# A hybrid decoder layer on one core: where the additions of the early down-projection chunks stand, when a third block sum is split, and which later chunks use seven products

## The chip, the cores and the metric

One core of one Trainium2 chip. The metric is the device time of one launch in microseconds (us), taken as the median of several executions; before the change it is 1123.89 us (three executions, 1123.33 to 1124.59). The profile is one further execution, recorded by the hardware profiler.

## The reference

One decoder layer on `x` of 256 tokens by 2048 features, float32:

```
proj = h @ w_in                                  # 2048 x 6144
a_out = diff_attention(8 heads); b_out = moba_attention(8 heads)   # with 256 tokens: causal attention
h = layer_norm(alpha * h + concat(a_out, b_out) @ w_out)
u = h @ w_up;  g, val = u[:, :5632], u[:, 5632:]
f = (silu(conv_b + causal 3-tap depthwise conv(g)) * val) @ w_down # 5632 x 2048
h = layer_norm(alpha * h + f)
```

The change concerns the last matrix product, `act @ w_down`, and the additions that bring its result into the residual.

## The kernel before

**Precision.** Every float32 operand of a large product is split into a high part `hi` (ScalarE copies it to the matmul format) and a low part `lo` (VectorE subtracts, `lo = x - hi`); a product is then hi·hi + hi·lo + lo·hi. So each weight tile costs one copy on ScalarE (ACT) and one subtraction on VectorE (DVE) before TensorE (PE) can use it.

**Stages.** Values, then queries, keys and attention, then the output projection and the first norm; then 88 *units* of the up projection (a unit is one 128-wide column of `w_up`: even ones gate, odd ones value; counted from 0, `i - first_u` in the code), then 14 *down chunks* at the end and the last norm. Instructions are written out by hand in one order per engine; each engine takes its own list in order and waits on semaphores.

**A unit** (`up_step`). PE does 16 pairs of matmuls (512 and 256 columns wide) into one bank, `bank[3]`. Then it does a slice of a *down job* (below). At the unit's end ACT copies the bank out (`up_copy`, tile `ub`, L1175); the next unit's first matmul writes the same bank, so it waits for that copy. In the same unit ACT and DVE split the weights of the unit after the next one (`hi` L190, `lo` L198), finish the gate of the unit before (`up_sum` L1184, taps L561/L562, product L568), and prepare the down job's operands.

**A down job.** `w_down` is taken in chunks: 256 of its rows (a pair `p`, 0 to 21) by 1024 of its columns (a half `n`). A chunk's product is a 2x2 by 2x2 block product done in seven block products instead of eight (Strassen's idea in Winograd's form): 21 matmuls of 512 columns, where the ordinary way takes 24. For that DVE forms sums of the weight blocks. Line by line: `tf` L1301 (block 0 minus block 3), `tf` L1309 (3 plus 2), `tf` L1317 (the *third sum*, 2 minus the first), `tf` L1269 (the fourth); each is split into `tslot` (high part by ACT at L803, low part by DVE at L806). The job also needs the plain blocks split (`rslot`, L1362 and L1364) and, for a chunk seen for the first time ("fresh"), sums of the activations (`sf`, split into `sp`, L809 and L812). The list `jobs` gives each job's half, pair, first unit, and its length in units, four or two. The sums of job j+1 are formed while job j runs; its third sum comes in the last unit of job j, behind everything else, just ahead of that unit's copy `ub`.

**Banks of the down jobs.** Each of the seven products adds up over the chunks in its own PSUM bank: MB[5], MB[7], MB[6], MB[1] (banks 5, 7, 6, 4) for the shared ones, and CB[0][0], CB[0][1], CB[1][0] (banks 0, 1, 2). The first ten jobs (`EARLY`) do half n=1 of pairs 0 to 9; then the banks have to be added into the residual `z` and given over to half n=0, all 20 remaining jobs. This handing over is the *flush*. Before the change it is eleven additions on DVE (L1211, L1223, L1226) and one copy on ACT, at the heads of units 46, 47 and 48 (`shared_out(1, ...)` and three additions of the CB banks), and job 10 is four units long (46 to 49), with no products in unit 46 so that the banks can be emptied. Job 9 is two units long (44 and 45).

**The down chunks at the end.** Chunks 0 and 1 are half n=0 of pairs 20 and 21, chunks 2 to 13 are half n=1 of the pairs not done early (index j of the code is the chunk's number minus 2). Chunk by chunk, `begin` splits the weights of the chunk two ahead and loads the one six ahead. The raw weights pass through four tiles in turn, so the load of chunk c+4 can be issued only when chunk c's raw tile is free; SyncE (SP) issues the loads in order. Most chunks are ordinary (24 matmuls); those that the table `SEVEN` names use seven products, whose raw tile is held until `blocks_whole` has read it (L666, L667), after all block sums. Before, these are chunks 5 and 8 (j = 3 and 6). The split tiles hold three ordinary chunks at a time. The last four chunks are taken column by column, all four for one bank, before the next bank.

Of the kernel before, what the change touches and what calls it, by code (L numbers as in the profile page):

```python
# [11 lines left out]
F32 = mybir.dt.float32  # L12
F32R = mybir.dt.float32r
AF = mybir.ActivationFunctionType
ALU = mybir.AluOpType

P = 128
# [29 lines left out]
LATE = 2  # L47

EARLY = 10

SEVEN = {"v": ((), range(1, 8, 3)), "d": (range(PT - LATE), (3, 6))}

ORDER = {"v": (1, 0, 2, 3), "d": (0, 1, 2, 3)}

# [5 lines left out]
def hymba_layer(ctx: ExitStack, tc: tile.TileContext, a: dict):  # L60
# [260 lines left out]
    def at(step, fn, *args, rank=LATER):  # L321
        after.setdefault(step, []).append((rank, len(after.get(step, ())), fn, args))
# [411 lines left out]

    side, raw0 = {}, {}

    jobs = []
    for p in range(EARLY):
        jobs.append((1, p, 4 * p + 8, 2 if p == EARLY - 1 else 4))
    jobs.append((0, 0, 4 * EARLY + 6, 4))  # L740
    for p in range(EARLY, PT - LATE):
        jobs.append((0, p, 4 * p + 10, 2))
        if p - EARLY + 1 < EARLY:
            jobs.append((0, p - EARLY + 1, 4 * p + 12, 2))
    FLUSH = EARLY

    def fresh(j):
        return jobs[j][1] >= EARLY or jobs[j][0] == 1
# [53 lines left out]
    def t_hi(j, f):  # L802
        ACT.activation(side["t"][:, 0, j], f, AF.Copy)  # L803

    def t_lo(j, f):
        DVE.tensor_tensor(side["t"][:, 1, j], f, side["t"][:, 0, j].bitcast(F32), ALU.subtract)  # L806

    def s_hi(j):
        ACT.activation(side["sh"][j], side["s"][j], AF.Copy)  # L809

    def s_lo(j):
        DVE.tensor_tensor(side["sl"][j], side["s"][j], side["sh"][j].bitcast(F32), ALU.subtract)  # L812
# [385 lines left out]
    def cuts(j, u):  # L1198

        _, _, first, length = jobs[j]  # L1200
        if length == 2:
            c = (0, 9, 21)
        elif j == FLUSH:
            c = (0, 0, 7, 14, 21)
        else:
            c = (0, 5, 10, 15, 21)
        return c[u - first], c[u - first + 1]

    def z_add(n, t, c, src):
        s = slice((2 * n + c) * 512, (2 * n + c + 1) * 512)  # L1210
        DVE.tensor_tensor(z[:, t, s], z[:, t, s], src, ALU.add)  # L1211

    def shared_out(n, part, early=False):

        if part == 0:
            kept["u"] = kept["gb"] if early else work.tile([P, 512], F32, name="u", tag="sh", bufs=1)
        u = kept["u"]
        if part == 0:
            ACT.activation(u, MB[1], AF.Copy)
            z_add(n, 0, 1, MB[5])  # L1220
            z_add(n, 1, 1, MB[5])
            z_add(n, 0, 0, u)
            DVE.tensor_tensor(u, MB[6], u, ALU.add)  # L1223
        else:
            z_add(n, 0, 1, u)
            DVE.tensor_tensor(u, MB[7], u, ALU.add)  # L1226
            z_add(n, 1, 0, u)
            z_add(n, 1, 1, u)

    def up_step(i):  # L1230

# [14 lines left out]
        if i > first_u + 2:  # L1246
            u = up_sum(i - 1)
            if s % 2 == 0:
                act_out(f, u)
        if j == FLUSH and 0 in now:  # L1250
            shared_out(1, 0, True)
        if j == FLUSH and 1 in now:
            shared_out(1, 1, True)
        if j == FLUSH and 2 in now:
            for t, c in ((1, 0), (0, 0), (0, 1)):
                z_add(1, t, c, CB[t][c])
        split_hi(i + 2, 0)
        if s % 2 == 1 and u is not None:
            gate_in(f, u)
# [55 lines left out]
        if 3 in nxt:  # L1315
            w = raw_of(j + 1)
            DVE.tensor_tensor(side["f"][0], w[:, 2], side["f"][0], ALU.subtract)  # L1317
            if fresh(j + 1):
                s_hi(0)
            t_hi(2, side["f"][0])  # L1320
            if fresh(j + 1):
                s_lo(0)
            t_lo(2, side["f"][0])
        if i == first_d - 2:
            split_act(first_d, 0)
        if i == first_d - 1:
# [71 lines left out]
    for i in range(first_d, NS - PAIRED_END):  # L1398
        begin(i)
        _, p, n, j = stream[i]  # L1400
        if i == last[0] - 1:
            act_back(last[3])
            ends = (down_slot()[:, 0:8].rearrange("p (a b) c -> p a (b c)", b=2),
                    keep.tile([P, 4, 1024], F32R, name="end", tag="mb"))
            for j, end in zip(last[2:], ends):
                for k in range(2):
                    split(j, k, end)
            for part in range(2):
                shared_out(1, part)
        if seven(i):  # L1410
            mm_seven(i)
        else:
            for k in range(2):
                mm_d(i, 0, [0, 1], k)
            if n == 0 and p == PT - 1:
                for c in range(2):
                    z_add(0, 0, c, CB[0][c])
            elif i < last[0] - 1:
                middle(i)
            for k in range(2):  # L1420
                mm_d(i, 1, [0, 1], k)
            done(i)
            if n == 0 and p == PT - 1:
                for c in range(2):
                    z_add(0, 1, c, CB[1][c])
                middle(i)
                for t in range(2):
                    for c in range(2):
                        at(i + 4 + 3 * t, z_stats, t, c, (512, 256)[t])
        for k in range(2):  # L1430
            aparts.pop((i, k))

# [171 lines left out]
```

## Time and profile before

| | |
|---|---|
| median of three executions | 1123.89 us |
| the profiled execution | 1124.31 us |
| its span, first to last instruction | 1122.5 us |
| PE busy | 1106.5 us (99%) |
| DVE busy | 889.0 us (79%) |
| ACT busy | 692.2 us (62%) |
| mean granted PE clock | 0.995 |
| down jobs: a unit with 9 products, one with 12 | 7.61 us, 8.28 us |

The profiled execution's own time is 1.8 us above its span. In the views, PE is TensorE's matmuls and PEld its weight loads; a row of a timeline gives the start, the duration, engine, line, operation and tiles, and in brackets how long the engine was idle before and what released it. PE's matmuls overlap, and their ends are modelled, so a busy share of 99% does not say that PE lost nothing: lost time is read from the starts of matmuls and from how long a unit took.

### The profile page before, as it was taken

How to read it: one execution, taken by the hardware profiler on the slowest of the kernel's cores; microseconds unless marked ns; L12 is line 12 of the kernel's file. 1: busy time of each engine (PE TensorE's matmuls, PEld its weight loads, DVE VectorE, ACT ScalarE, POOL GpSimd, SP SyncE). 2: the span in 40 equal slices, each digit the busy share in tenths (PEclk: the TensorE clock that was granted, in tenths of full speed). 3: DMA queues.
4: the chain of work that ended last, by engine and by line, in shares of the span. 5: the costliest groups of instructions: out<-in, count | busy, mean ns of one | idle time of the engine just before them, and what ended most of it. 6: DMA issues, size and time to landing. Idle time of an engine off the chain costs nothing.

```text
span 1122.5 us, 15881 instructions
## 1 busy us (share of the span) xinstructions
PE 1106.5 (99%) x5908; PEld 949.5 (85%) x5908; DVE 889.0 (79%) x1470; ACT 692.2 (62%) x1109; POOL 61.8 (6%) x88
## 2 busy tenths in 40 slices
PE   9999999999999999999999999899999999999997
PEld 7888888888888898888888888788888888888876
DVE  6776778877745779888888878888888888886876
ACT  6666666655443577666666666566676666666452
POOL 0000010000000000000000000000000000001003
PEclk9999999999999999999999999999999999999998
DMA  9889866454545447888787888578888777798772
GB/s 344 273 276 325 227 195 201 150 187 156 183 168 200 157 166 264 279 271 277 271 273 262 292 266 286 187 262 300 277 269 267 252 281 269 262 307 284 245 268 76
DMA packets 61884, 273.80 MB, mean 244 GB/s; under 512 B 6304, under 2 KB 7792, under 8 KB 44016
## 3 DMA queue, kind: packets, MB, share of 16 engines
q1 hardware_dynamic: 52592, 233.48, 57.1%
q0 software_dynamic: 9072, 39.06, 15.3%
q8 instruction: 46, 0.75, 0.3%
q10 hardware_dynamic: 144, 0.26, 0.1%
q14 instruction: 30, 0.25, 0.1%
HBM read 231.60 MB, written 18.87 MB: 223 GB/s over the span
## 4 chain that ended last, share of the span: by engine, by line
PE 84%; DVE 8%; ACT 4%; issue 2%; DMA 2%; SPq 0%; ACTq 0%; DVEq 0%
PE bank L279 83%; DVE lo L198 1%; DVE rslot L1364 1%; ACT ub L1175 1%; DMA raw<-in_w_d 1%; ACT rslot L1362 1%; ACT hi L190 1%; DVE z L1211 1%; ACT tslot L803 1%; DVE tf L1309 1%; DVE tf L1317 1%; PE bank L421 0%; DVE lo L181 0%; DMA raw<-in_w_v 0%; DVE gc L562 0%
## 5 line engine op out<-in xcount | busy, mean ns | idle before, releaser
L279 PE MATMUL bank<-h,hi 128*128 128x512 f32 x1376 | 483.5, 392 | 4.7 <-ACT ub L1175 3.6
L279 PE MATMUL bank<-h,lo 128*128 128x256 f32 x1376 | 388.4, 282 | 0.0
L279 PEld LDWEIGHTS bank<-h,hi 128*128 128x128 f32 x1376 | 258.9, 188 | 63.8 <-ACT ub L1175 9.3
L279 PEld LDWEIGHTS bank<-h,lo 128*128 128x128 f32 x1376 | 260.6, 189 | 3.2
L198 DVE TENSOR_TENSOR lo<-raw,hi 128x1024 fp32r<-128x1024 f32 x171 | 207.6, 1220 | 19.8 <-ACT hi L190 19.6
L181 DVE TENSOR_TENSOR lo<-raw,hi 128x1024 fp32r<-128x1024 f32 x133 | 160.3, 1221 | 70.9 <-ACT hi L179 70.1
L179 ACT ACTIVATE hi<-raw 128x1024 fp32r<-128x1024 f32 x141 | 147.6, 1057 | 67.1 <-PE bank L279 46.5
L279 PE MATMUL bank<-x,hi 128*128 128x512 f32 x512 | 182.8, 398 | 0.0
L190 ACT ACTIVATE hi<-raw 128x1024 fp32r<-128x1024 f32 x171 | 178.2, 1050 | 0.0
L279 PE MATMUL bank<-x,lo 128*128 128x256 f32 x512 | 144.1, 282 | 0.0
L803 ACT ACTIVATE tslot<-tf 128x512 fp32r<-128x512 f32 x120 | 74.4, 627 | 76.9 <-DVE tf L1317 35.4
L279 PEld LDWEIGHTS bank<-x,hi 128*128 128x128 f32 x512 | 96.1, 188 | 20.6 <-issue 1.0
L1175 ACT ACTIVATE ub<-bank 128x512 f32<-128x512 f32 x86 | 51.1, 594 | 92.0 <-PE bank L279 92.0
L806 DVE TENSOR_TENSOR tslot<-tf,tslot 128x512 fp32r<-128x512 f32 x120 | 82.0, 690 | 23.2 <-ACT tslot L803 21.3
L279 PEld LDWEIGHTS bank<-x,lo 128*128 128x128 f32 x512 | 96.8, 189 | 0.2
L1184 DVE TENSOR_TENSOR ub<-ub 128x256 f32<-128x256 f32 x86 | 36.3, 422 | 28.1 <-ACT ub L1175 28.0
L279 PE MATMUL bank<-hi,x 128*128 128x512 f32 x208 | 55.9, 391 | 0.1
L279 PEld LDWEIGHTS bank<-hi,x 128*128 128x128 f32 x208 | 38.9, 188 | 8.9 <-ACT hi L210 0.9
L279 PE MATMUL bank<-tslot,sp 128*128 128x512 f32 x180 | 45.9, 391 | 0.0
L279 PE MATMUL bank<-hi,mh 128*128 128x512 f32 x128 | 41.6, 396 | 0.0
L565 ACT ACTIVATE gc<-gc 128x256 f32<-128x256 f32 x44 | 18.4, 418 | 36.8 <-DVE gc L562 36.8
L279 PE MATMUL bank<-lo,mh 128*128 128x512 f32 x128 | 40.8, 390 | 0.0
(246 smaller groups left out, 1532.1 us busy)
## 6 DMA issues: line engine op xcount, KB each, us to landing
raw<-in_w_u SPq DMA_DIRECT2D x88, 1024.0 KB, 6.8
raw<-in_w_qk SPq DMA_DIRECT2D x32, 1024.0 KB, 5.0
raw<-in_w_d SPq DMA_DIRECT2D x58, 512.0 KB, 7.9
raw<-in_w_o SPq DMA_DIRECT2D x16, 1024.0 KB, 4.8
ring<-in_w_d SPq DMA_DIRECT2D x30, 512.0 KB, 8.4
raw<-in_w_v SPq DMA_DIRECT2D x28, 512.0 KB, 7.4
rslot<-ring POOLq DMA_DIRECT2D x15, 768.0 KB, 7.0
dparts<-rslot SPq DMA_DIRECT2D x20, 512.0 KB, 3.8
```

Of the source, the lines that this page charges most:

```text
L179: ACT.activation(hi[:, s], t[:, x:y], AF.Copy)
L181: DVE.tensor_tensor(lo[:, s], t[:, x:y], hi[:, s].bitcast(F32), ALU.subtract)
L190: ACT.activation(hi, t[:, half * 1024:half * 1024 + 1024], AF.Copy)
L198: DVE.tensor_tensor(lo, t[:, half * 1024:half * 1024 + 1024], hi.bitcast(F32), ALU.subtract)
L279: PE.matmul(out, lhsT, rhs, start=start, stop=stop)
L565: ACT.activation(gates[f], gates[f], AF.Silu)
L803: ACT.activation(side["t"][:, 0, j], f, AF.Copy)
L806: DVE.tensor_tensor(side["t"][:, 1, j], f, side["t"][:, 0, j].bitcast(F32), ALU.subtract)
L1175: ACT.activation(t.rearrange("p j t -> p (j t)"), up_bank(i), AF.Copy)
L1184: DVE.tensor_tensor(u[:, 0], u[:, 0], u[:, 1], ALU.add)
L1211: DVE.tensor_tensor(z[:, t, s], z[:, t, s], src, ALU.add)
L1309: DVE.tensor_tensor(side["f"][1], w[:, 3], w[:, 2], ALU.add)
```

## The change

Four things.

1. `jobs`: job 9 is four units long (44 to 47) instead of two, and job 10 two (48 and 49) instead of four. From unit 50 on the jobs stand where they stood.
2. The flush is rewritten as `early_out(0)` to `early_out(3)`, in units 46, 47, 48 (at the end of the unit's list) and 49 (near its head). It has 13 additions on DVE instead of 11 (MB[1] is added to all four quarters of `z` directly, and the running sum `u` starts from a copy of MB[6]) and still one copy on ACT.
3. `third_out`: where job j+1 is two units long, the split of its third sum (and of the fresh job's first activation sum) is not done in the last unit of job j but is carried to the head of the next unit, behind `up_sum` and `act_out`. The sum itself (L1317, now L1335) stays.
4. `SEVEN`: among the end's chunks only chunk 6 (j = 4) uses seven products, not chunks 5 and 8. Two z statistics move one chunk later.

```diff
-SEVEN = {"v": ((), range(1, 8, 3)), "d": (range(PT - LATE), (3, 6))}
+SEVEN = {"v": ((), range(1, 8, 3)), "d": (range(PT - LATE), (4,))}
...
-    jobs = []
+    jobs = [(1, p, 4 * p + 8, 4) for p in range(EARLY)]
     for p in range(EARLY):
-        jobs.append((1, p, 4 * p + 8, 2 if p == EARLY - 1 else 4))
-    jobs.append((0, 0, 4 * EARLY + 6, 4))
-    for p in range(EARLY, PT - LATE):
-        jobs.append((0, p, 4 * p + 10, 2))
-        if p - EARLY + 1 < EARLY:
-            jobs.append((0, p - EARLY + 1, 4 * p + 12, 2))
-    FLUSH = EARLY
+        jobs += [(0, p, 4 * (EARLY + p) + 8, 2), (0, EARLY + p, 4 * (EARLY + p) + 10, 2)]
...
+    flush = 4 * EARLY + 6
+    carried = []
+
+    def early_out(part):
+
+        u = kept["gb"]
+        if part == 0:
+            z_add(1, 0, 1, MB[5])
+            z_add(1, 1, 1, MB[5])
+            ACT.activation(u, MB[6], AF.Copy)
+            z_add(1, 0, 1, MB[6])
+        elif part == 1:
+            DVE.tensor_tensor(u, MB[7], u, ALU.add)
+            z_add(1, 1, 0, u)
+            z_add(1, 1, 1, u)
+            z_add(1, 1, 0, CB[1][0])
+        elif part == 2:
+            for t in range(2):
+                for c in range(2):
+                    z_add(1, t, c, MB[1])
+        else:
+            for c in range(2):
+                z_add(1, 0, c, CB[0][c])
+
+    def third_out(j):
+        if fresh(j):
+            s_hi(0)
+        t_hi(2, side["f"][0])
+        if fresh(j):
+            s_lo(0)
+        t_lo(2, side["f"][0])
...
-        if j == FLUSH and 0 in now:
-            shared_out(1, 0, True)
-        if j == FLUSH and 1 in now:
-            shared_out(1, 1, True)
-        if j == FLUSH and 2 in now:
-            for t, c in ((1, 0), (0, 0), (0, 1)):
-                z_add(1, t, c, CB[t][c])
+        if i - first_u == flush + 3:
+            early_out(3)
+        if carried:
+            carried.pop()()
         split_hi(i + 2, 0)
...
             DVE.tensor_tensor(side["f"][0], w[:, 2], side["f"][0], ALU.subtract)
-            if fresh(j + 1):
-                s_hi(0)
-            t_hi(2, side["f"][0])
-            if fresh(j + 1):
-                s_lo(0)
-            t_lo(2, side["f"][0])
+            if jobs[j + 1][3] == 4:
+                third_out(j + 1)
+            else:
+                carried.append(lambda: third_out(j + 1))
+        if flush <= i - first_u < flush + 3:
+            early_out(i - first_u - flush)
...
-                        at(i + 4 + 3 * t, z_stats, t, c, (512, 256)[t])
+                        at(i + 5 + 2 * t, z_stats, t, c, (512, 256)[t])
```

How the instructions stand, at the three places that matter most. First ACT's list from unit 53 into unit 54, before (`tslot` from `tf_3873` in the fifth row is the third sum's high part, `sp` the activation sum, `ub` the copy that frees PE's bank):

```order
L1362 ACTIVATE rslot_4030<-raw_6599 128x1024
L803 ACTIVATE tslot_3872<-tf_3873 128x512
L803 ACTIVATE tslot_3872<-tf_3874 128x512
L809 ACTIVATE sp_3877<-sf_3875 128x256
L803 ACTIVATE tslot_3872<-tf_3873 128x512
L1175 ACTIVATE ub_6897<-bank3_74 128x512
L190 ACTIVATE hi_6933<-raw_6742 128x1024
```

The same place after (L797 is the old L803, L803 the old L809, L1169 the old L1175):

```order
L1380 ACTIVATE rslot_4030<-raw_6592 128x1024
L797 ACTIVATE tslot_3872<-tf_3873 128x512
L797 ACTIVATE tslot_3872<-tf_3874 128x512
L1169 ACTIVATE ub_6894<-bank3_74 128x512
L803 ACTIVATE sp_3877<-sf_3875 128x256
L797 ACTIVATE tslot_3872<-tf_3873 128x512
L190 ACTIVATE hi_6934<-raw_6741 128x1024
```

The activation sum and the third sum now stand behind the copy instead of ahead of it.

Second, DVE's list at the flush. Before, the head of unit 48, where the three CB banks (2, 0, 1) are added ahead of the weight splits L198:

```order
L1184 TENSOR_TENSOR ub_6483<-ub_6483 128x256
L568 TENSOR_TENSOR ring_3714<-ub_6483,gc_6458 128x256
L1211 TENSOR_TENSOR z_80<-z_80,bank2_73 128x512
L1211 TENSOR_TENSOR z_80<-z_80,bank0_71 128x512
L1211 TENSOR_TENSOR z_80<-z_80,bank1_72 128x512
L198 TENSOR_TENSOR lo_6523<-raw_6348,hi_6522 128x1024
L198 TENSOR_TENSOR lo_6527<-raw_6348,hi_6526 128x1024
L1364 TENSOR_TENSOR rslot_4030<-raw_6205,rslot_4030 128x1024
```

After, the end of unit 48 and the head of unit 49 (L1178 is `up_sum`, L1200 an addition into `z`, bank 4 is MB[1]):

```order
L1319 TENSOR_TENSOR tf_3873<-ring_3714 128x512
L811 TENSOR_TENSOR sf_3875<-ring_3714 128x256
L812 TENSOR_TENSOR sf_3876<-sf_3875,ring_3714 128x128
L813 TENSOR_TENSOR sf_3876<-ring_3714,sf_3876 128x128
L1200 TENSOR_TENSOR z_80<-z_80,bank4_75 128x512 x4
L1178 TENSOR_TENSOR ub_6534<-ub_6534 128x256
L1200 TENSOR_TENSOR z_80<-z_80,bank0_71 128x512
L1200 TENSOR_TENSOR z_80<-z_80,bank1_72 128x512
L198 TENSOR_TENSOR lo_6572<-raw_6394,hi_6571 128x1024
```

The additions of MB[1] end unit 48's list; those of banks 0 and 1 open unit 49's. Ahead of these, and not shown, three additions end unit 46's list and four end unit 47's.

Third, DVE's list among the end's chunks. Before, around the end of chunk 8's block sums (`raw_9423` is chunk 8, `raw_9464` chunk 9, `raw_9514` chunk 10; `slot` holds the seven-product blocks):

```order
L676 TENSOR_TENSOR tf_9578<-raw_9423,tf_9578 128x512
L181 TENSOR_TENSOR lo_9623<-raw_9464,hi_9622 128x1024
L659 TENSOR_TENSOR slot_9456<-tf_9578,slot_9456 128x512
L667 TENSOR_TENSOR slot_9456<-raw_9423,slot_9456 128x1536
L181 TENSOR_TENSOR lo_9647<-raw_9514,hi_9646 128x1024
```

After, from the end of chunk 6's block sums on (`raw_9345` is chunk 6, `raw_9422` chunk 8, `raw_9466` chunk 9, `raw_9505` chunk 10):

```order
L667 TENSOR_TENSOR slot_9497<-raw_9345,slot_9497 128x1536
L181 TENSOR_TENSOR lo_9567<-raw_9422,hi_9566 128x1024
L181 TENSOR_TENSOR lo_9583<-raw_9422,hi_9582 128x1024
L1394 BN_STATS st512_9590<-z_80 128x6 x2
L181 TENSOR_TENSOR lo_9603<-raw_9466,hi_9602 128x1024
L181 TENSOR_TENSOR lo_9619<-raw_9466,hi_9618 128x1024
L181 TENSOR_TENSOR lo_9639<-raw_9505,hi_9638 128x1024
```

The last block of a seven-product chunk that is read raw (L667) moves from just ahead of chunk 10's split to just ahead of chunk 8's; chunks 8 to 13 are split the ordinary way, one behind the other.

More of the change, by code (lines that the diff above doesn't have):

```diff
@@ L1200, in cuts @@
         _, _, first, length = jobs[j]
[L1201 to L1206, printed above, removed]
+        c = (0, 9, 21) if length == 2 else (0, 5, 10, 15, 21)
         return c[u - first], c[u - first + 1]
@@ L1211, in z_add, with shared_out @@
         DVE.tensor_tensor(z[:, t, s], z[:, t, s], src, ALU.add)
-    def shared_out(n, part, early=False):
+    def shared_out(n, part):
         if part == 0:
-            kept["u"] = kept["gb"] if early else work.tile([P, 512], F32, name="u", tag="sh", bufs=1)
+            kept["u"] = work.tile([P, 512], F32, name="u", tag="sh", bufs=1)
         u = kept["u"]
```

## The prediction

> **What bounds the kernel now.** I read the totals, then who makes PE wait, then the time of single units, then the chain and timelines at the places found. Totals and PE's two longest waits in sum (columns: total us, times, longest):
>
> ```profile
> span 1122.5 us, 15881 instructions
> ...
> PE bank L279 <- ACT ub L1175: 3.6, 2, 2.9
> PE bank L279 <- ACT end L179: 1.6, 1, 1.6
> ```
>
> PE is the bound, and so few waits look like nothing to gain. But a modelled matmul end hides short waits, and waits lower the granted clock. So I take whole units: PE time by stretch (columns: length, busy, granted clock, DMA share, GB/s). The first four rows are units 46 to 49 (0, 7, 7 and 7 products), the next four units 54 to 57 (9, 12, 9, 12 products), the last four the clock around PE's two long waits:
>
> ```profile
> 694.86:701.32 6.46, 5.71 (x34) 1.00 0.82 331
> 701.32:708.58 7.26, 7.26 (x40) 1.00 0.42 144
> 708.58:718.76 10.18, 7.30 (x40) 0.98 0.49 157
> 718.76:727.43 8.67, 8.67 (x39) 0.82 0.83 301
> 791.67:799.38 7.71, 7.71 (x42) 1.00 0.97 270
> 799.38:807.66 8.28, 8.28 (x45) 1.00 1.01 361
> 807.66:815.27 7.61, 7.61 (x42) 1.00 0.87 326
> 815.27:823.84 8.57, 8.45 (x46) 1.00 0.41 136
> 718.40:721.80 3.40, 3.04 (x9) 0.50 0.96 355
> 1093.90:1097.30 3.40, 3.40 (x9) 0.50 0.02 5
> 715.00:718.40 3.40, 0.88 (x4) 1.00 0.49 118
> 1090.50:1093.90 3.40, 1.07 (x3) 1.00 0.00 0
> ```
>
> An undisturbed unit takes 7.61 us with 9 products and 8.28 with 12, so a product costs 0.67/3 = 0.223 and 16 pairs alone 7.61 - 9 x 0.223 = 5.60. With that there are three losses.
>
> *The flush.* Units 46 to 49 should take 5.60 and three times 5.60 + 7 x 0.223 = 7.16. They lose 0.86, 0.10, 3.02 and 1.51, together 5.5 us. The 1.51 is the clock: after a stretch in which PE was busy for 0.88 of 3.40, it was granted half, and 3.04 us of work at half rate cost 1.5.
>
> *Every fourth unit.* Unit 57 takes 8.57 instead of 8.28, and the start of unit 54 (after such a one) 7.71 instead of 7.61: 0.39 us. The chain shows how often. Its pieces (start, length, what) at the flush, then the first and the last of the copies through which it later passes:
>
> ```profile
> 711.62 1.87 DVE z L1211 x3
> 713.49 2.27 DVE lo L198 x2
> 715.76 1.14 DVE rslot L1364
> ...
> 718.13 0.59 ACT ub L1175
> 718.76 30.29 PE bank L279 x156
> ...
> 758.86 0.59 ACT ub L1175
> ...
> 1016.27 0.59 ACT ub L1175
> ```
>
> From 758.86 to 1016.27 is 257.4 us, eight periods of 32.17 (the four units' sum), so nine such places, 3.5 us in all. What holds the copy up, at the end of unit 57:
>
> ```profile
> 820.61 0.63 ACT L803 ACTIVATE tslot<-tf 128x512 fp32r<-128x512 f32 x1 [1.43 <-DVE tf L1309]
> ...
> 821.51 2.20 PE L279 MATMUL bank<-rslot,more 128*128 128x512 f32 x9
> 821.89 0.69 DVE L1317 TENSOR_TENSOR tf<-ring,tf 128x512 f32<-128x512 f32 x1
> ...
> 822.67 0.64 ACT L803 ACTIVATE tslot<-tf 128x512 fp32r<-128x512 f32 x1 [1.12 <-DVE tf L1317]
> 823.21 0.58 ACT L1175 ACTIVATE ub<-bank 128x512 f32<-128x512 f32 x1
> ```
>
> The bank was full when the products began, yet the copy runs at 823.21, since ACT's list has the third sum's split ahead of it, and that waits for DVE's L1317. PE's last nine products start at 821.51 and fill 9 x 0.223 = 2.0 us, so PE is ready at 823.5; the copy ends at 823.79.
>
> *The end.* Chunk 13's weights come late. The load of chunk 8 (first SP row), of chunk 13 (second), the last block of chunk 5 read raw, and PE and ACT at the last chunk; then DMA by stretch (length, clock, DMA share, GB/s) and the size of one of a chunk's two loads:
>
> ```profile
> 1047.34 0.38 SPq L128 DMA_DIRECT2D raw<-in_w_d  x1
> ...
> 1078.54 0.38 SPq L128 DMA_DIRECT2D raw<-in_w_d  x1
> ...
> 1061.30 1.76 DVE L667 TENSOR_TENSOR slot<-raw,slot 128x1536 fp32r<-128x1536 f32 x1 [0.35 <-ACT slot L666]
> ...
> 1088.86 1.63 PE L279 MATMUL bank<-slot,back 128*128 128x512 f32 x6
> 1090.97 2.00 ACT L179 ACTIVATE end<-raw 128x1024 fp32r<-128x1024 f32 x2 [3.16 <-DMA raw<-in_w_d]
> ...
> 1093.33 1.19 PE L279 MATMUL bank<-end,slot 128*128 128x512 f32 x3 [0.76 <-DVE end L181]
> ...
> 1054.00:1062.00 8.00, 1.00 0.04 6
> 1063.00:1079.00 16.00, 1.00 0.94 333
> ...
> raw<-in_w_d SPq DMA_DIRECT2D x58, 512.0 KB, 7.9
> ```
>
> Chunk 5 uses seven products, and its raw tile is free only when L667 ends at 1063.06. SP's next load stands behind that, so DMA is idle from 1054 to 1062, and then five chunks' loads come in two bursts. PE had six products to do from 1088.86 and one of the last chunk, 7 x 0.223 = 1.56, and should have gone on at 1090.42; it went on at 1093.33, 2.9 us late, and then ran 3.40 us at half rate, 1.7 more: 4.6 us.
>
> **The change part by part.** *Third split carried.* Nothing is added; a copy on ACT and a subtraction on DVE (and for a fresh job the same for a smaller `sp`) move behind `ub`. The copy is then free after the second sum's split, 820.61 + 0.63 = 821.24, ends at 821.8 and leaves 1.7 us to 823.5. The wait goes: -3.5. What is late next: the carried split must be done before its products, which PE reaches 5.60 us into the next unit, plus 6 x 0.223 for the third sum's own. L1317 ends at 822.58, and `up_sum`, `act_out` and the two subtractions take about 0.42 + 0.42 + 0.42 + 0.69 behind it: done near 824.6, one microsecond into the unit. ACT's additional work there, at most two times 0.64, lies ahead of a copy that PE does not release before 5.60. I take 0 for this cost; it cannot be below, since PE goes no faster than its products; from the other side, if the wait only moved, it is 3.5.
>
> *Ten first chunks' flush.* Products stay the same in number: units 44 to 49 now have 5, 5, 5, 6, 9, 12. So the question is DVE. Effective costs from the chain: 512 columns 1.87/3 = 0.62, 1024 columns 1.14. The small ones by these rows (busy, mean ns, idle before; the second is a tap):
>
> ```profile
> L1184 DVE TENSOR_TENSOR ub<-ub 128x256 f32<-128x256 f32 x5 | 2.1, 421 | 2.2 <-ACT ub L1175 2.2
> ...
> L561 DVE SCALAR_TENSOR_TENSOR gc<-ub,vec,gc 128x255 f32<-128x255 f32 x2 | 1.0, 478 | 0.0
> ```
>
> Unit 46: two small, two splits at 1.14, one sum, two sum splits, three additions: 0.84 + 2.28 + 6 x 0.62 = 6.8 us against PE's 5.60 + 5 x 0.223 = 6.7. Unit 47: `up_sum`, two taps, two splits, five wide: 0.42 + 0.96 + 2.28 + 3.1 = 6.8 against 6.9. DVE only just keeps pace. Unit 48: two small, two splits, third and fourth sum's work (three wide), block 0's low part, next job's first sum, three activation sums (at most 0.42 each, I take 1.0), four additions: 0.84 + 2.28 + 9 x 0.62 + 1.0 = 9.7, and about 0.5 of waiting for ACT's copy of block 0: 10.2 against 7.6. So DVE enters unit 49's list 2.7 us late (0.1 brought along). There come `up_sum`, two additions, two splits, two taps, the low parts of blocks 1 and 2 (1.14) and the next second sum: 0.42 + 1.24 + 2.28 + 0.96 + 1.14 + 0.62 = 6.7. Only then can ACT split that sum (0.63) and make the copy (0.58). That copy ends 2.7 + 6.7 + 1.2 = 10.6 us after the unit's start, about 10.8 with the hops between engines; PE is due at 8.28. PE loses some 2.6 us, in pieces: about 2 waiting for blocks 1 and 2 in the midst of unit 49's products, the rest for the copy. Unit 50's DVE list then starts late, but unit 51 has room: `up_sum`, two splits, two taps and four wide are 0.42 + 2.28 + 0.96 + 2.48 = 6.1 us against 8.28. So the flush costs 2.6 instead of 5.5: -2.9. The bounds are 0 (gain 5.5) and, with the clock halved once, 4.1 (gain 1.4).
>
> Clock: the trace halved it after PE had been busy 0.88 and 1.07 of 3.40 us. In the new flush no stretch of 3.4 us should have less than about 1.4 busy. The Trainium skill (TensorE: Matmul & The Clock Gate, "Why this matters for your kernels") advises to avoid idle gaps above some 3 us between bursts; by that alone waits in pieces under 2 us would cost nothing beyond themselves and the sum stays. The trace speaks against that: gaps of 1.6 and 0.8 with matmuls between them were enough at 1092. So a halved clock is kept as a rival.
>
> *One seven-product chunk.* Three more products: +0.7. Chunk 5 becomes ordinary, so the load behind it is issued when its plain split is done, ahead of all block sums, and the idle stretch of DMA is used. Chunk 6's blocks follow one chunk later: if they end as much later as a chunk is long (24 x 0.223 = 5.4), at 1068.5 at the latest, rather near 1066, as DVE has one chunk's sums less ahead. Then two splits, two statistics and two splits, about 5.8 us, and chunk 13's load goes out at 1072 to 1074 instead of 1078.5. Four chunks of 1 MB and about 1 MB of activations read back at 333 GB/s from 1066 to 1068.5 take 16 us: landed by 1082 to 1084.5. PE needs it at 1090.4 + 0.7, ACT's copy (2.00/2) and DVE's low part (1.14) before that: 1089.0. Four us are left, so the 4.6 go, less 0.7: -3.9. What covers the +0.7: nothing, PE is the bound. If chunk 13 is as late as before, the part costs 0.7.
>
> Sum: 2.9 + 3.5 + 3.9 = 10.3 off the profiled execution's 1124.31 (span 1122.5 and 1.8 around it): 1114.0. That execution is 0.4 above the median 1123.89, so the median should come to 1113.6.
>
> **The rivals.** *Halved clock at the flush:* for it, the trace's two cases; against it, the waits are broken up by products. One stretch at half rate costs 1.5: 1115.1.
>
> *The change doesn't remove the every-fourth wait* but moves it: the carried split, at the head of DVE's and ACT's lists, delays another thing that PE waits for. For it, DVE's head of unit 54 is then one long row of work; against it, 1.7 us of room at the old place and four us at the new one. Plus 3.5: 1117.1.
>
> *The last load stays late,* since the burst behind chunk 6 saturates DMA: plus 4.6, 1118.2. For it, 333 GB/s from 1063 to 1079 already; against it, the idle 8 us ahead are put to use, one MB less is left over.
>
> *The flush hides fully:* DVE keeps pace better than I count, 2.6 less: 1111.0.
>
> *Slower:* the carried split turns DVE into the bound of every four units. DVE then must take its subtraction behind ACT's high part at the head of units, and each of the two carried splits in a period waits up to 0.7 for it. Undisturbed, a period is 2 x (7.61 + 8.28) = 31.8 us. If DVE's list became longer than that by 1.4 (1.0 more than today's 32.17), nine periods lose 12.6, and the time is 1113.6 + 12.6 = 1126.2. It decides from the point where added waiting exceeds DVE's free time in the period; against it, the same list passes today in 32.17 with the copy's wait in it.
>
> **How the numbers follow.** Forecast 0.49; halved clock 0.24; wait moved 0.09; late load 0.08; flush hidden 0.05; slower 0.05. The predicted time is the forecast's, 1113.6. Its sums carry about 0.8 us either way from the flush's estimate; the range from 1112.4 to 1117.6 holds the forecast, the halved clock and the moved wait, 0.82 in all. 0.2% is 2.2 us, about what a measurement can tell from no change. All cases but the last are faster by more than that; between them lie combinations (late load with halved clock and moved wait) that come near no change: faster 0.91, same 0.04, slower 0.05.
>
> **What would show it.** Right: units 46 to 48 at 6.7, 6.9 and 7.6 us; unit 49 near 10.9 with PE waiting in its products for `rslot`; unit 57 at 8.28 and its copy within 1 us of the products' start; chunk 13's load some 5 us earlier against the end of the up projection than now; no wait of PE on `end`, and full clock there. Wrong: 0.50 in the granted clock after unit 49; a wait for `ub` at the end of a unit with `tslot` ahead of it; a copy `end` released by a DMA; units 54 to 57 above 31.8 us.

## The result, and the profile after

The changed kernel takes 1114.44 us (median of four executions, 1114.16 to 1115.7) against 1123.61 for the kernel before (four beside it, 1123.14 to 1124.59). The ratio is 0.9919, with a 95% interval of 0.9902 to 0.9937: 9.2 us less, between 7.1 and 11.0. The forecast was 1113.6. The profiled execution took 1114.31 us, 10.0 less than the profiled one of before; 10.3 were forecast.

To see where it came from, I cut both spans at the start of unit 44, at the start of unit 50 and at chunk 0. PE time by these three stretches, of the kernel before (columns: length, PE busy, then the weight loads and the other engines, granted clock, DMA share, GB/s):

```profile
678.97:727.43 48.46, 44.84 (x235) 38.43 (x234) 41.43 (x64) 28.32 (x43) 1.99 (x3) 0.96 0.72 243
727.43:1032.90 305.47, 304.36 (x1616) 260.97 (x1615) 259.86 (x407) 206.94 (x317) 18.62 (x28) 1.00 0.82 271
1032.90:1122.50 89.60, 80.50 (x362) 65.05 (x360) 65.41 (x94) 35.54 (x45) 15.53 (x20) 0.95 0.59 210
```

and of the changed kernel:

```profile
679.23:724.70 45.47, 43.64 (x236) 37.14 (x234) 40.19 (x61) 26.86 (x41) 1.98 (x3) 1.00 0.64 218
724.70:1026.78 302.08, 302.08 (x1616) 261.93 (x1616) 262.13 (x412) 208.82 (x319) 18.56 (x28) 1.00 0.83 278
1026.78:1112.30 85.52, 78.67 (x365) 64.71 (x363) 60.96 (x87) 33.55 (x42) 15.00 (x19) 0.97 0.59 214
```

The flush gave 48.46 - 45.47 = 3.0, the units behind it 305.47 - 302.08 = 3.4, the end 89.60 - 85.52 = 4.1. The forecast's three terms were 2.9, 3.5 and 3.9. (Up to unit 44 this execution is 679.23 - 678.97 = 0.3 behind; with that the spans differ by 10.2.)

Units 46 to 49 of the changed kernel, then unit 57:

```profile
692.63:699.33 6.70, 6.70 (x38) 5.86 (x37) 6.45 (x10) 5.02 (x8) 0.00 (x0) 1.00 1.02 419
699.33:706.26 6.93, 6.93 (x40) 6.04 (x38) 6.65 (x11) 3.70 (x7) 0.00 (x0) 1.00 0.81 278
706.26:713.87 7.61, 7.61 (x43) 6.61 (x42) 7.04 (x13) 4.54 (x6) 0.00 (x0) 1.00 0.26 79
713.87:724.70 10.83, 9.00 (x46) 6.91 (x44) 10.28 (x16) 4.61 (x8) 0.00 (x0) 1.00 0.28 103
780.10:788.39 8.29, 8.29 (x46) 7.18 (x45) 7.70 (x12) 5.46 (x10) 0.00 (x0) 1.00 0.37 121
```

Units 46 to 49 take 6.70, 6.93, 7.61 and 10.83 us, where 6.7, 6.9, 7.6 and 10.9 were forecast, and unit 57 takes what 12 products take. PE's waits behind 600 us, and the end of unit 49 on DVE and ACT:

```profile
PE bank L279 <- DVE rslot L1382: 0.8, 1, 0.8
PE bank L279 <- ACT rslot L1380: 0.7, 1, 0.7
...
PE bank L279 <- ACT ub L1169: 0.4, 1, 0.4
```

```profile
721.61 1.23 DVE L1382 TENSOR_TENSOR rslot<-raw,rslot 128x1024 fp32r<-128x1024 f32 x1 [0.35 <-ACT rslot L1380]
...
722.75 0.69 DVE L1327 TENSOR_TENSOR tf<-ring 128x512 f32<-128x512 f32 x1
...
723.53 0.64 ACT L797 ACTIVATE tslot<-tf 128x512 fp32r<-128x512 f32 x1 [1.43 <-DVE tf L1327]
724.07 0.58 ACT L1169 ACTIVATE ub<-bank 128x512 f32<-128x512 f32 x1
```

The chain is the forecast's: low part, second sum, its split, copy. The copy ends at 724.65, 10.8 us after the unit's start. In the steady part the copy of unit 57 stands ahead of the split of the third sum (L1335), not behind it:

```profile
785.98 0.58 ACT L1169 ACTIVATE ub<-bank 128x512 f32<-128x512 f32 x1
...
787.43 0.64 ACT L797 ACTIVATE tslot<-tf 128x512 fp32r<-128x512 f32 x1 [0.57 <-DVE tf L1335]
```

At the end: the first half of chunk 13's load, the copy `end` (no wait for a DMA ahead of it) and the last chunk on PE (no wait either), then a stretch in which DMA is quiet:

```profile
1065.70 0.38 SPq L128 DMA_DIRECT2D raw<-in_w_d  x1
...
1078.84 1.99 ACT L179 ACTIVATE end<-raw 128x1024 fp32r<-128x1024 f32 x2
...
1084.58 1.52 PE L279 MATMUL bank<-end,slot 128*128 128x512 f32 x6
...
1052.00:1061.00 9.00, 9.00 (x41) 7.45 (x40) 7.57 (x9) 7.34 (x9) 1.06 (x2) 1.00 0.18 58
```

The load goes out 1065.70 - 1026.78 = 38.9 us behind chunk 0's start; before it was 1078.54 - 1032.90 = 45.6. But the quiet stretch of DMA has not gone: it is there from 1052 to 1061, at a share of 0.18.

### The profile page after: what moved, and what is told of

Same layout as the page of the kernel before. It is cut to its first block, busy times and chain, and to the rows that moved or that the text cites. A ratio compares the mean times of both kernels' runs of the same rounds, so it can differ in the third digit from the quotient of the medians.

```text
span 1112.3 us, 15875 instructions
## 1 busy us (share of the span) xinstructions
PE 1101.4 (99%) x5911; PEld 949.1 (85%) x5911; DVE 885.9 (80%) x1465; ACT 690.6 (62%) x1106; POOL 61.1 (5%) x87
## 4 chain that ended last, share of the span: by engine, by line
PE 96%; DVE 2%; ACT 1%; DMA 0%; issue 0%; SPq 0%; DVEq 0%; ACTq 0%
PE bank L279 95%; PE bank L421 0%; DMA raw<-in_w_v 0%; DVE z L1200 0%; DVE lo L198 0%; PE bank L1049 0%; PE bank L468 0%; ACT hf L1052 0%; ACT rslot L1380 0%; DVE h L1064 0%; ACT tslot L797 0%; DVE rslot L1382 0%; DVE st L492 0%; DVE z L489 0%; ACT hi L190 0%
## 5 line engine op out<-in xcount | busy, mean ns | idle before, releaser
L198 DVE TENSOR_TENSOR lo<-raw,hi 128x1024 fp32r<-128x1024 f32 x171 | 207.7, 1221 | 20.1 <-ACT hi L190 19.8
L1169 ACT ACTIVATE ub<-bank 128x512 f32<-128x512 f32 x86 | 51.2, 596 | 106.9 <-PE bank L279 106.9
L797 ACT ACTIVATE tslot<-tf 128x512 fp32r<-128x512 f32 x120 | 74.4, 627 | 52.5 <-DVE tf L1327 27.6
L1178 DVE TENSOR_TENSOR ub<-ub 128x256 f32<-128x256 f32 x86 | 36.4, 423 | 32.1 <-ACT ub L1169 32.0
L279 PEld LDWEIGHTS bank<-hi,x 128*128 128x128 f32 x208 | 38.9, 188 | 9.2 <-ACT hi L210 1.2
L279 PE MATMUL bank<-hi,ml 128*128 128x512 f32 x128 | 40.8, 390 | 0.0
```

The source lines that it names most:

```text
L198: DVE.tensor_tensor(lo, t[:, half * 1024:half * 1024 + 1024], hi.bitcast(F32), ALU.subtract)
L279: PE.matmul(out, lhsT, rhs, start=start, stop=stop)
L1169: ACT.activation(t.rearrange("p j t -> p (j t)"), up_bank(i), AF.Copy)
L1178: DVE.tensor_tensor(u[:, 0], u[:, 0], u[:, 1], ALU.add)
```

## The experiments

Twelve kernels, each timed in five rounds beside the kernel before (medians 1123.6 to 1124.6). The last column is the ratio's distance from 1 in us.

| kernel | median us | ratio, 95% interval | difference us |
|---|---|---|---|
| carry: carried split alone | 1120.87 | 0.9974 (0.9965 to 0.9984) | -2.9 |
| seven: one seven-product chunk alone | 1120.77 | 0.9968 (0.9955 to 0.9980) | -3.6 |
| flush: jobs and flush alone | 1125.89 | 1.0017 (1.0008 to 1.0025) | +1.9 |
| nocarry: all but the carried split | 1122.75 | 0.9989 (0.9980 to 0.9998) | -1.2 |
| f50: all but job 11's carried split | 1118.29 | 0.9953 (0.9938 to 0.9968) | -5.3 |
| j6: chunk 8 on seven products | 1114.65 | 0.9919 (0.9905 to 0.9933) | -9.1 |
| j3: chunk 5 on seven products | 1114.82 | 0.9916 (0.9900 to 0.9933) | -9.4 |
| j24: chunks 4 and 6 | 1123.63 | 1.0001 (0.9992 to 1.0010) | +0.1 |
| j25: chunks 4 and 7 | 1119.87 | 0.9959 (0.9947 to 0.9972) | -4.6 |
| pool: four additions on POOL | 1117.22 | 0.9945 (0.9931 to 0.9959) | -6.2 |
| ahead: flush one unit earlier | 1113.42 | 0.9914 (0.9900 to 0.9929) | -9.7 |
| acopy: ahead, and the copy earlier | 1112.96 | 0.9896 (0.9883 to 0.9910) | -11.7 |

### The parts one by one

**carry**, from the kernel before:

```
...
+        if carried:
+            carried.pop()()
...
+            if jobs[j + 1][3] == 4 or j + 1 <= FLUSH:
+                third_out(j + 1)
+            else:
+                carried.append(lambda: third_out(j + 1))
```

> The kernel before with one part of the change alone: where the next job is two units long, the split of its third sum is carried to the head of the next unit (jobs, flush and seven-product chunks as before). Theory (nine waits of 0.39 us for the copy `ub` behind this split go, and nothing is late in their place): 3.5 us less than before, 1120.1, unit 57 at 8.28 us. Rival (the wait only moves to something that the carried split delays): within 0.5 us of before, 1123.6, with another tile behind `tslot` in PE's waits.

2.9 us less (1.8 to 3.9): the theory. Unit 57 takes what 12 products take, and nothing is late in place of the old wait:

```profile
784.01:792.30 8.29, 8.29 (x45) 7.17 (x44) 7.70 (x12) 5.45 (x10) 0.00 (x0) 1.00 0.38 124
```

From unit 50 (728.73) to chunk 0 (1030.69) this trace takes 301.96 us, 3.5 less than before. It loses 1.3 again in unit 49, which takes 10.01 us instead of 8.67. Units 46 to 48 take the same as before, but the windows of the clock (last section) lie otherwise: it is at half rate from 717.91 to 724.74, twice as long. So the clock can be what is missing to 3.5 in the median; what the other executions lost there is not known.

**seven**, from the kernel before:

```
-"d": (range(PT - LATE), (3, 6))
+"d": (range(PT - LATE), (4,))
...
-                        at(i + 4 + 3 * t, z_stats, t, c, (512, 256)[t])
+                        at(i + 5 + 2 * t, z_stats, t, c, (512, 256)[t])
```

> The kernel before with chunk 6 alone on seven products in the place of chunks 5 and 8 (and the two statistics of z one chunk later), nothing else. Theory (the wait of 2.9 us for the last chunk and the 1.7 us at half clock behind it go, three products more cost 0.7): 3.9 us less, 1119.7, no wait on `end`. Rival (the last load stays late, since the transfers behind chunk 6 fill DMA): 0.7 us more than before, 1124.3, with the wait on `end` still there.

3.6 us less (2.2 to 5.1), and `end` is not among PE's waits: the theory again.

**flush**, from the changed kernel, with `(3, 6)` and its statistics back, and

```
-            if jobs[j + 1][3] == 4:
-                third_out(j + 1)
-            else:
-                carried.append(lambda: third_out(j + 1))
+            third_out(j + 1)
```

> The kernel before with the new job lengths (job 9 four units, job 10 two) and the new additions of the ten first chunks' banks, but the third split where it was and chunks 5 and 8 on seven products. Theory (flush loses 2.6 us in place of 5.5): 2.9 us less, 1120.7; unit 49 may lose up to 0.6 more than in the changed kernel, since the third split of job 11 then stands ahead of its copy: 1121.3 at most. Rival (without the carried split the flush gains nothing, since DVE's list in unit 49 and the copy behind it are what PE waits for): 1123 or more. Rival (the clock is halved after unit 49): 1122.2.

1.9 us *more*. The theory falls by 4.8 us. The time lies in the first rival's range (1123 or more), and its place is the right one, as the rows below show: the copy behind DVE's list in unit 49. But it counted on no gain, and not on a loss; the halved clock of the second rival comes on top. Units 49 and 50 of this kernel, and 3.4-us windows of it:

```profile
713.81:727.35 13.54, 9.02 (x46) 6.91 (x44) 12.50 (x21) 5.55 (x10) 0.00 (x0) 0.96 0.41 131
727.35:737.65 10.30, 10.30 (x41) 8.80 (x42) 6.85 (x13) 6.96 (x11) 1.97 (x3) 0.72 0.98 265
719.35:722.77 3.42, 2.03 (x9) 1.14 (x7) 3.03 (x5) 1.89 (x3) 0.00 (x0) 1.00 0.00 0
722.77:726.18 3.41, 1.45 (x5) 0.86 (x5) 3.25 (x6) 0.94 (x3) 0.00 (x0) 1.00 0.40 105
726.18:729.59 3.41, 2.25 (x7) 1.96 (x8) 2.96 (x6) 3.41 (x5) 0.00 (x0) 0.50 0.98 380
729.59:733.00 3.41, 3.41 (x12) 2.89 (x11) 2.78 (x6) 2.93 (x7) 1.97 (x3) 0.50 0.91 245
```

Unit 49 is 13.54 - 10.83 = 2.7 us longer than in the changed kernel, and unit 50 10.30 against 7.6 for its work, since the clock is halved from 726.18 to 733.00. What stands in the way, in units 47 and 49:

```profile
704.54 0.69 DVE L800 TENSOR_TENSOR tslot<-tf,tslot 128x512 fp32r<-128x512 f32 x1 [0.70 <-ACT tslot L797]
...
726.18 0.63 ACT L797 ACTIVATE tslot<-tf 128x512 fp32r<-128x512 f32 x1 [1.11 <-DVE tf L1335]
726.71 0.58 ACT L1169 ACTIVATE ub<-bank 128x512 f32<-128x512 f32 x1
```

In unit 47 DVE stands idle for 0.70 us for ACT's half of job 10's third split, and enters unit 49's list 0.6 later (717.05, not 716.45). In unit 49 the copy stands behind job 11's third split, which waits for DVE's L1335. So the copy runs at 726.71, not at 724.07. The new flush makes DVE late just where the old place of the third split makes ACT wait for DVE.

**nocarry** asks the same with chunk 6 alone on seven products, so with all other parts in: the changed kernel with `third_out(j + 1)` always at once (the last diff, alone).

> The changed kernel with no third split carried (the parts `jobs`, flush and one seven-product chunk stay). Theory (the carry and the new flush hang together: beside the nine waits, the carry keeps the split of job 11 out of the way of unit 49's copy and that of job 10 out of DVE's late list, which the flush alone showed): 3.1 us under the kernel with the flush alone, which was at 1125.9, so 1122.8. Rival (the parts are independent, and the carry is worth the 2.9 us that it gained alone): 1117.3.

1122.75: the theory to 0.1 us, and 5.5 from the rival. The carried split was worth 2.9 us alone and 1122.75 - 1114.44 = 8.3 in this kernel.

**f50** puts one of the carried splits back:

```
-            if jobs[j + 1][3] == 4:
+            if jobs[j + 1][3] == 4 or j == EARLY:
```

> The changed kernel with one third split put back: job 11's is done in unit 49 again and not carried to unit 50; all others are carried. The flush alone had lost 4.8 us more than forecast. Theory (most of that is this split: in unit 49, where DVE is late, it stands ahead of the copy `ub`, PE then waits some 2.4 us more for the copy, 2.58 + 0.37 against 0.55, and the longer stretch of little work halves the clock for another 1.5): 3.9 us more than the changed kernel, 1118.3, with 0.50 in the granted clock after unit 49. Rival (the loss came from job 10's split in unit 47, whose 0.7 us of DVE waiting for ACT delays the low part in unit 49): within 0.5 us of the changed kernel, 1114.4.

The median is 1118.29, as the theory had it; the rival, no loss, falls. But the profiled execution is one of the short ones (1116.19), and shows only the waiting half of it, with the clock at full rate although PE was busy for just 0.98 us from 723.50 to 726.91. The rows are PE's wait, and the two stretches of 3.41 us into which the clock's windows (last section) divide this place:

```profile
PE bank L279 <- ACT ub L1169: 2.4, 1, 2.4
...
721.58:724.99 3.41, 1.93 (x6) 1.05 (x6) 3.16 (x5) 1.52 (x4) 0.00 (x0) 1.00 0.26 57
724.99:728.40 3.41, 1.58 (x9) 1.41 (x10) 2.95 (x7) 2.75 (x4) 0.00 (x0) 1.00 1.02 347
```

Its six executions fall apart: 1116.19 and 1116.39, and four from 1118.01 to 1119.26. The mean granted clock is recorded with each: 0.998 for the two short ones, 0.997 or 0.994 for the four others. So these four did lose clock; no trace shows where, and that it was behind unit 49 is argued.

### The end

**j6** and **j3**, from the changed kernel, with `(6,)` and with `(3,)` in the place of `(4,)`.

> The changed kernel with chunk 8 in the place of chunk 6 on seven products. It tells apart two readings of why the end's wait went. Gate (what made chunk 13's load late before was that SP stands in order behind the raw tile that a late seven-product chunk holds; chunk 8 holds it longest and nearest to the end): the wait on `end` comes back, with 2 to 4.6 us, 1116.4 to 1119.0. Throughput (what went is only the amount left to load behind the idle stretch of DMA; one seven-product chunk instead of two is enough wherever it stands): no wait, within 0.5 us of the changed kernel, 1114.4.

> The changed kernel with chunk 5 in the place of chunk 6 on seven products. Chunk 8 alone had left no wait on `end`. Theory (the last load was late only where both holds came, chunk 5's, which leaves DMA idle and five loads for a burst, and chunk 8's, behind which the last two loads stand; either alone is harmless): no wait on `end`, within 0.7 us of the changed kernel, 1114.4. Rival (chunk 5's hold with its idle stretch of DMA is the cause by itself, as the prediction's step had it): the wait comes back with at least 1.5 us and the clock behind it, 1116.5 or more.

Neither has a wait on `end`: 1114.65 in j6, where the reading called gate misses and the time is that of the other, and 1114.82 in j3, the theory. In j6 the last two loads do stand behind chunk 8's block, and the copy does wait for its DMA, but the split of chunk 13 is done at 1081.34 + 2.36 = 1083.70 and PE comes at 1085.04:

```profile
1067.88 1.76 DVE L667 TENSOR_TENSOR slot<-raw,slot 128x1536 fp32r<-128x1536 f32 x1 [0.35 <-ACT slot L666]
...
1070.65 0.38 SPq L128 DMA_DIRECT2D raw<-in_w_d  x1
1080.24 2.01 ACT L179 ACTIVATE end<-raw 128x1024 fp32r<-128x1024 f32 x2 [2.84 <-DMA raw<-in_w_d]
1081.34 2.36 DVE L181 TENSOR_TENSOR end<-raw,end 128x1024 fp32r<-128x1024 f32 x2 [2.48 <-ACT end L179]
...
1085.04 1.52 PE L279 MATMUL bank<-end,slot 128*128 128x512 f32 x6
```

In j3 the quiet stretch of DMA stands where it stood before, in front of chunk 5's block, and does no harm:

```profile
1046.00:1057.00 11.00, 11.00 (x51) 9.06 (x49) 9.50 (x12) 6.13 (x7) 0.53 (x1) 1.00 0.19 61
```

So it took both holds: chunk 5's, which bunched the loads, and chunk 8's, behind which the last two then stood. Chunk 13's load went out 45.6 us behind chunk 0's start before and 1070.65 - 1027.24 = 43.4 in j6, and its copy began 1090.97 - 1078.54 = 12.4 us behind the load before and 9.6 in j6. The kernels carry and flush, which keep both holds, keep the wait on `end` too (1.4 and 0.8 us, 1.0 and 0.8). The rival "chunk 5's idle stretch by itself" falls, and so does "chunk 8's hold by itself".

**j24** and **j25** ask whether two holds can be had earlier: `(2, 4)` and `(2, 5)` in the place of `(4,)`.

> The changed kernel with chunks 4 and 6 on seven products, not chunk 6 alone: three products fewer, and two raw tiles held long as in the kernel before, but earlier in the stage. Theory (the last load was late only because both holds came late, at chunks 5 and 8, and five loads were left for the time behind the first): no wait on `end`, 3 x 0.223 = 0.7 us less, 1113.7. Rival (two holds are too much for the loads wherever they stand): the wait comes back with at least 1 us and the clock behind it, 1115.5 or more.

> The changed kernel with chunks 4 and 7 on seven products, three chunks apart as in the kernel before but one chunk earlier each, so that the two don't share their split blocks at once. Theory (two holds are too much only where the second comes so late that the last two loads stand behind it; here three loads stand behind chunk 7 and leave it one chunk, 5.4 us, earlier): no wait on `end`, three products less, 0.7 us under the changed kernel, 1113.7. Rival (two holds are too much wherever they stand): a wait on `end` of 1 us or more and the clock behind it, 1115.5 or more.

Both miss, for reasons that neither theory names. PE's longest wait in j24, and in j25:

```profile
PE bank L279 <- ACT slot L652: 7.4, 1, 7.4
```

```profile
PE bank L279 <- DVE u L1215: 4.2, 1, 4.2
```

In j24 the copy that PE waits for is this one:

```profile
1055.63 1.23 ACT L652 ACTIVATE slot<-tf 128x512 fp32r<-128x512 f32 x2 [5.14 <-DVE tf L649]
```

It splits the first two block sums of chunk 6, and in the order of the program it stands ahead of chunk 4's products, since each step first splits the chunk two ahead. Both chunks use the one set of split blocks `slot`, and the same place for their activation sums. So chunk 4's products wait for chunk 6's blocks and multiply by them: j24 does not compute the layer, and its time says nothing of two holds. Three chunks apart this can't happen, but chunk 4's products need MB[7] while the first half's sums are still being added from it (L1215 of `shared_out(0, ...)`); PE, idle for a whole window there, was then at half rate for 3.41 us more. Neither has a wait on `end`, but PE was held up before, so for two holds with PE on time the question stays open.

### What is left of the flush

**pool**, from the changed kernel (`z_pool` is `z_add` on POOL):

```
...
-            for t in range(2):
-                for c in range(2):
-                    z_add(1, t, c, MB[1])
+            ACT.activation(u, MB[1], AF.Copy)
+            for c in range(2):
+                z_pool(1, 1, c, u)
         else:
             for c in range(2):
                 z_add(1, 0, c, CB[0][c])
+                z_pool(1, 0, c, u)
```

> The changed kernel with the four additions of MB[1] taken off DVE: ACT copies the bank to the free tile `gb` in unit 48, and POOL adds the copy to the four quarters of z, two in unit 48, two behind the CB additions in unit 49. Theory (DVE's list is what makes PE wait in unit 49, so 4 x 0.62 = 2.5 us less on DVE take nearly all of the 2.64 us away): 1112.0, with `rslot` no longer among PE's waits. Rival (what PE waits for is ACT behind the stage, or POOL's additions hold up DVE by as much as they take off it): 1114.4 or more.

2.8 us slower than the changed kernel: the rival. The first two of POOL's additions, and DVE beside all four:

```profile
711.22 3.55 POOL L1221 TENSOR_TENSOR z<-z,ring 128x512 f32<-128x512 f32 x2 [28.00 <-ACT ring L1240]
711.31 2.32 DVE L198 TENSOR_TENSOR lo<-raw,hi 128x1024 fp32r<-128x1024 f32 x1
713.54 1.78 DVE L1324 TENSOR_TENSOR tf<-ring 128x512 f32<-128x512 f32 x1
...
717.76 1.95 DVE L198 TENSOR_TENSOR lo<-raw,hi 128x1024 fp32r<-128x1024 f32 x1
719.63 1.51 DVE L561 SCALAR_TENSOR_TENSOR gc<-ub,vec,gc 128x255 f32<-128x255 f32 x1
...
721.17 0.48 DVE L562 SCALAR_TENSOR_TENSOR gc<-ub,vec,gc 128x254 f32<-128x254 f32 x1
721.57 1.22 DVE L198 TENSOR_TENSOR lo<-raw,hi 128x1024 fp32r<-128x1024 f32 x1
```

The last two rows are DVE without POOL: 0.48 and 1.22, and a sum like L1324 took 0.69 above (L1327). Beside POOL the four DVE rows took 1.10 + 1.09 + 0.73 + 1.03 = 3.95 us more. Four additions at 0.62 came off, 2.5. So DVE's list became 1.5 longer, and PE's wait for `rslot` grew with it:

```profile
PE bank L279 <- ACT rslot L1385: 2.2, 1, 2.2
```

This wait was 0.7 in the changed kernel: 1.5 more, which is nearly all of this execution's 1115.66 - 1114.31 = 1.35. It was the shortest of six; the others, from 1116.65 to 1117.71, have a mean granted clock of 0.995 or 0.996 on record, and this one 0.997. So the rest of the 2.8 goes with a lower clock, in executions of which no trace shows the place.

**ahead**, from the changed kernel:

```
-        c = (0, 9, 21) if length == 2 else (0, 5, 10, 15, 21)
+        c = (0, 9, 21) if length == 2 else (0, 9, 12, 15, 21) if j == EARLY - 1 else (0, 5, 10, 15, 21)
...
-    flush = 4 * EARLY + 6
+    flush = 4 * EARLY + 5
```

> The changed kernel with the flush one unit earlier: job 9's products are cut 9, 3, 3, 6 over units 44 to 47 (not 5, 5, 5, 6), so that the additions stand at the ends of units 45, 46, 47 and the head of 48, with none in unit 49. DVE was busy 4.68 of 6.70 and 5.09 of 6.70 us in units 44 and 45, and without a pause from 699 to 731 us. Theory (the same 13 additions use the idle time of unit 45; three of them fewer stand between unit 46 and the low part that PE waits for: 3 x 0.62 = 1.9 us off a loss of 2.64): 1112.6. Rival (the gain is lost in units 46 and 47, whose lists become longer than PE's work, so PE waits there for split weights or for the copy): 1114.0 or more.

1113.42 (1113.03 to 1114.07): 1.0 less than the changed kernel, whose shortest execution was 1114.16 (against the kernel before, the two intervals overlap). The theory's direction, with half of its size. PE's waits there are down from 0.8 + 0.7 + 0.4 to 0.7, 0.3 for `rslot` and, as before, 0.4 for the copy. By the units, unit 49 takes 9.43 us instead of 10.83, 1.4 less; but units 45 to 47, with 3, 3 and 6 products, take 20.01 where their work is 6.27 + 6.27 + 6.94 = 19.48. So the rival is true in part: 0.5 of the gain is lost in the units that the additions moved to.

**acopy** moves that copy, from ahead:

```
             t_lo(0, side["f"][0])
+            if i - first_u == 4 * EARLY + 9:
+                up_copy(i)
             t_hi(1, side["f"][1])
...
-        up_copy(i)
+        if i not in halves:
+            up_copy(i)
```

> The kernel with the flush one unit earlier, and in unit 49 the copy `ub` stands on ACT ahead of the second split of the second sum (`tslot`), so that it no longer waits for DVE's L1327. Theory (PE's last wait there, 0.55 us at the start of unit 50, is for this place in ACT's list alone): 0.5 us under the kernel with the flush one unit earlier, which was at 1113.4, so 1112.9. Rival (the delayed split makes job 11's products late instead): no change, 1113.4.

1112.96 (1112.84 to 1113.12), as expected, and faster than both kernels: 11.7 us under before (10.1 to 13.2) and 1.5 under the changed one by the medians. `ub` is no longer among PE's waits, and the 0.3 for `rslot` is the only one left there. That is not all that the flush still costs: units 44 to 49 take 723.31 - 679.18 = 44.13 us, where 6 x 5.60 and 42 products of 0.223 are 42.97. Of the 2.5 us that the changed kernel loses there, 1.2 are left.

## Why the prediction was right, and where not

*The flush.* Right in size (3.0 against 2.9) and in its place: blocks 1 and 2 in the midst of unit 49's products, then the copy. DVE's list was worked out instruction by instruction for the order that stands in the changed kernel: DVE was to enter unit 49's list 2.7 us late, and its first instruction there starts at 716.45, 2.6 behind the unit's start. pool, ahead and acopy confirm that this list, and the place of the copy behind it, is what PE waits for.

*That the parts add up* was taken without a word, and it fails. The walk through units 48 and 49 had no third split in it, so the carried split was an unspoken condition of the 2.9. Alone, the new flush costs 1.9; without the carried split the whole change gains 1.2 in place of 9.2. The sum came out since it was made for the three parts together, not since the parts can be priced one by one.

*Every fourth unit.* 3.4 against 3.5, and alone 2.9 by the median and 3.5 in its own trace from unit 50 on, with nothing late in its place. The rival that the wait moves falls, and so does the slower one: four units take 788.39 - 756.60 = 31.8, the undisturbed period. The rows that the prediction calls units 54 to 57 are units 58 to 61, since unit 50 starts at 727.43; unit 57 itself took 791.67 - 783.11 = 8.56 before, so the period and the sum stay.

*The end.* 4.1 against 3.9, right in the load's time (6.7 us earlier against the stage, some 5 forecast). The step "the idle stretch of DMA is used" is wrong: the stretch only moved, one chunk later in the stage, with DMA's share at 0.18. j3 shows that it does no harm; what went is the coincidence of two holds. The rival of a late last load falls.

*The halved clock* did not come in the changed kernel, but not for the reason given. The prediction counted on at least 1.4 us of PE work in any 3.4 and took this as safe. The least in any such stretch of the changed kernel is more:

```profile
721.10:724.51 3.41, 1.92 (x6) 1.05 (x6) 2.90 (x5) 1.98 (x4) 0.00 (x0) 1.00 0.14 34
```

1.4 would not have been safe. In the flush kernel a window with 1.45 was followed by half rate; in nocarry one with 1.50 was:

```profile
720.10:723.51 3.41, 1.50 (x6) 0.68 (x4) 3.02 (x4) 1.89 (x3) 0.00 (x0) 1.00 0.00 0
723.51:726.92 3.41, 2.50 (x5) 1.49 (x5) 2.97 (x6) 1.47 (x3) 0.00 (x0) 0.50 0.58 136
726.92:730.33 3.41, 2.77 (x9) 2.39 (x10) 3.25 (x6) 3.41 (x6) 0.20 (x1) 0.50 1.05 428
730.33:733.74 3.41, 3.41 (x12) 2.92 (x12) 2.78 (x5) 2.40 (x5) 1.77 (x3) 0.50 0.88 195
```

So here the forecast was lucky: with the 1.4 that it counted on, the clock could have been halved, depending on where the windows lay; it stayed away because PE had 1.92 us of work. All four executions of the changed kernel have a mean granted clock of 0.998.

## What to carry to other kernels

An instruction that makes one engine wait for another costs little where there is slack and much where the other engine is late: cost each part of a change in the list it will stand in, and say which other parts that list presumes. Before moving work to an idle engine, look whether the two share something: POOL's additions cost DVE more than they saved. And where a late transfer has two causes in a row, taking away either may do; which one is the cheaper to give up is then free to choose.

## What the runs showed of the hardware

*The clock is judged in fixed windows.* The half-rate stretches of flush and nocarry last 733.00 - 726.18 = 6.82 and 733.74 - 723.51 = 10.23 us, two and three times 3.41. In the kernel before, the two halvings start at 718.43 and 1093.90, and the 375.47 between them are 110 times 3.413; in flush they start at 726.18 and, when the matmuls are over, at 1118.73, 115 times 3.413 later. So the windows go on through a whole execution. In f50 the clock goes to half rate at 1110.69, at the end, and its windows can be counted back from there: 113 and 114 of them earlier begin the two shown above, which split the stretch with 0.98 us of work, and in which PE was busy for 1.93 and 1.58. Where the windows lie differs from execution to execution, so the same instructions can lose the clock in one and not in another.

How busy PE must be is known only in part. At the flush, windows at full rate with PE busy for 1.45 and 1.50 us were followed by half rate, those with 1.58 and more were not. But in pool a window at the layer's end, 1104.79 to 1108.21, had 2.19 and was followed by half rate, so busy time alone, as the profile models it, is not the rule. Once at half rate, windows with 2.25, 2.50 and 2.77 busy kept it there; one that was full ended it, and in the kernel before one with 3.04.

The Trainium skill (TensorE: Matmul & The Clock Gate, "What's actually happening") describes a free-running window of 3413 ns, and these lengths agree. Its advice to keep idle gaps under some 3 us ("Why this matters for your kernels") is not enough here: in nocarry PE's longest wait ahead of the halving was 1.3 us, for `rslot`.

*POOL and DVE.* DVE's instructions with two operands in SBUF took 0.7 to 1.1 us more while POOL's additions ran, and two of these took 3.55 us. One of DVE's additions that read a bank stood beside POOL's by the profile's spans (717.17 to 717.85, POOL from 717.32) and took 0.68 us, as the one ahead of it did. The Trainium skill (SBUF — State Buffer, "Who interferes with whom") says that a DVE instruction with two SBUF inputs contends with a GpSimd instruction that reads SBUF; the rows of pool agree.
